# Seven half-size products for the values of four heads, with token forms made in the gelu branch

## The chip, the cores and the metric

The kernel runs on one core of a Trainium2 chip. The metric is the device time of one execution in microseconds. TensorE is written PE, VectorE DVE, ScalarE ACT, GpSimd POOL and SyncE SP, as in the profile.

## The reference

One layer over 528 tokens (16 meta tokens and 512 of the input), model width 1024, all in f32:

```python
h = concat([meta, x]); xn = rms_norm(h, norm_mix_g)
z = xn @ w_in
u_rnn, u_gate, q, k, v, g_ret, ga, gb = split(z)     # 1280, 1280, 1024, 1024, 2048, 2048, 1024, 1024
xr = causal_dwconv(u_rnn); hr = rg_lru(xr)           # two gates per block, then a scan over tokens
o_a = hr * gelu(u_gate)
q, k = rotary(q), rotary(k)                          # 4 heads, dk 256, dv 512
o_b = head_rms(retention(q, k, v)) * silu(g_ret)     # decayed scores, times the values
mixed = sigmoid(ga) * (o_a @ w_branch_rnn) + sigmoid(gb) * (o_b @ w_branch_ret)
h = h + mixed @ w_out
up = causal_dwconv(rms_norm(h, norm_ffn_g) @ w_up); gate, val = split(up)
out = rms_norm(h + (gelu(gate) * val) @ w_down, norm_final_g)[16:]
```

## The kernel before

**Products.** PE multiplies f16. Every f32 operand is cut into a high and a low f16 part (`split`: ACT writes the high part, DVE the low one as source times scale minus high), and a product is made as high x high, high x low and low x high (`SPLIT`, three matmuls). Channels lie on the partitions and tokens along the columns, as `xh`, `xl` for the normed input.

**Weights.** Weights come in units of 128 x 2048 f32. The list `units` gives their order. SP loads a unit into one of two `raw` tiles; its splits are steps that `get()` runs when a unit is needed and `tick()` runs between products, as far ahead as `ahead[0]` allows; a tile of `wsp` holds a split of up to 1024 elements. A plain unit has two splits of 128x1024. A fast unit serves a product of two-by-two blocks by seven half-size products (Strassen-Winograd): two splits of its own blocks (512 and 1024), three sums on DVE (1024, 512 and 512 elements, L256 to L258, which write into `raw`), and two late splits of 1024 (behind ScalarE's last copy). Such products also need four sums of the other operand, its forms, named F3, F5, F6 and F7. `fast_products` does the seven for a gate unit: four psum banks, ACT copies of a bank that is read while it goes on accumulating (`keep`), and DVE additions. ga and gb units and all gates g_ret were fast before the change, as were some of the FFN's.

**Stages on PE**, with their place in the trace: norm and first units to 33 us; the recurrent branch's convolution and gates to 84; the gelu branch, ten projections in the loop `for n in range(NR)`, to 138; between its projections the recurrent branch's gates, exponentials, square roots and scans run on ACT and DVE. Then the rotary projections q0, k0, ... q3, k3 (48 matmuls of 257 or 264 columns each, four psum tiles in turn; DVE gives a tile back with the additions L759 and L760) to 226; the scores and values of the heads, with retention and gates: scores(0) and values(0) from 226, then scores(1), scores(2), values(1), scores(3); from 285 retention_out(0), gated(0), values(2), gated(1), values(3), gated(2), to 420. The mixing (gates ga, gb, branch products, and head 3's gates among them) takes 420 to 690, the output projection to 720, the FFN's first matrix to 948 and its second to 1066.

**values(h).** The weights of a head's values are two plain units of four k blocks by 512 columns. For each of four blocks of 128 tokens, 24 matmuls hold the tokens still and move 512 weight columns (L930). The last 16 tokens have 16 small matmuls over four column groups (L922, `xlast`). Five splits make the values' f16 parts, and `flush()` stands between the blocks.

**make_forms.** The token forms for the gates are made in two halves g around scores(1) and scores(2): per half 12 instructions on DVE and four on ACT, of 514 elements.

**ob_forms.** The second branch's operands are made from the gated retention outputs in three steps for each unit; each step goes to `pending`, and `flush()` takes one. Before, `advance` flushes one after three of the seven products of a gate, `values` after each block.

**Order.** Up to `order.close()`, behind the gelu loop, instructions on an engine run in the order of the code (`manual_schedule`); after it a scheduler orders them per engine.

Of the kernel before, what the change touches and what calls it, by code (L numbers as in the profile page):

```python
# [8 lines left out]
F32 = mybir.dt.float32  # L9
# [17 lines left out]
TQ = T - T0  # L27
FAST_UP = (3, 5, 7, 9)
# [23 lines left out]
def hybrid_block_kernel(ctx, tc, x, meta, norm_mix_g, w_in, conv_w, conv_b, rg_a_w, rg_a_b,  # L52
# [7 lines left out]
    wsp = ctx.enter_context(tc.tile_pool(name="wsp", bufs=10))  # L60
# [67 lines left out]
    def add_v(h):  # L128
        u_v[h] = [unit(4, 512, [(0, 0, kmaj(w_in, 4 * a, 4, o_v + 512 * h, 512))]) for a in range(2)]
# [699 lines left out]
    x_form_t = {}  # L829

    def make_forms(g):

        if not x_form_t:
            for i in range(2):
                x_form_t[i] = xslot([P, 4, 4, 257], F16, f"xs{i}")
        ks = slice(2 * g, 2 * g + 2)
        t = {}
        for i in range(2):
            for j in range(2):
                v = t[i, j] = wtile("xt")[:, :TQ].rearrange("p (k c) -> p k c", k=2)  # L840
                k0, (c0, n) = 4 * j + 2 * g, HQ[i]
                nc.vector.tensor_tensor(v, xh[:, k0:k0 + 2, c0:c0 + n], xl[:, k0:k0 + 2, c0:c0 + n], op=ALU.add)
        a11, a12, a21, a22 = t[0, 0], t[0, 1], t[1, 0], t[1, 1]
        nc.vector.tensor_tensor(a22, a22, a21, op=ALU.subtract)
        nc.vector.tensor_tensor(a21, a11, a21, op=ALU.subtract)
        nc.vector.scalar_tensor_tensor(a11, a22, -1.0, a11, op0=ALU.mult, op1=ALU.subtract)
        nc.vector.scalar_tensor_tensor(a12, a11, -1.0, a12, op0=ALU.mult, op1=ALU.subtract)
        for i, v in enumerate((a12, a22, a11, a21)):
            xs = x_form_t[i // 2]
            split(xs[:, 2 * (i % 2), ks], xs[:, 2 * (i % 2) + 1, ks], v, 1.0)  # L850

    def x_forms(nm, a, k):
        if nm[0] == "A":
            c0, n = HQ[int(nm[1]) - 1]
            return xf(a, 4 * (int(nm[2]) - 1) + k, c0, n)
# [51 lines left out]
    def values(h):  # L907
        vt = []
        wa, wb = get(u_v[h][0]), get(u_v[h][1])
        for b, (j0, nb) in enumerate(JB):  # L910
            if h >= 2 or b % 2 == 0:
                ps = acc("ps")
# [763 lines left out]
```

## Time and profile before

| | |
|---|---|
| median of 3 runs | 1067.75 us (1067.13 to 1067.86) |
| span of the profiled execution | 1066.5 us, 1.25 us below the median of the runs; its mean clock is 0.998 |
| PE busy | 1048.0 us, 98% |
| DVE busy | 853.2 us, 80% |
| ACT busy | 587.9 us, 55% |
| HBM | 108.04 MB read, 103 GB/s over the span |

In the profile a row of groups has line, engine, operation, out<-in, shape and count, then busy time and mean ns of one, then the engine's idle time just before and what ended it. A timeline row has start and length; rows overlap a little where instructions are pipelined, so a pitch is taken from start to start. A number in brackets is idle time before the row and what ended it.

### The profile page before, as it was taken

The page shows a single profiled execution, that of the slowest core. Times are in us where ns is not written, and L with a number is a line of the kernel's source. Part 1 is how long each engine was busy: PE and PEld are TensorE (multiplying, and loading weights), DVE is VectorE, ACT ScalarE, POOL GpSimd, SP SyncE. Part 2 cuts the span into 40 slices and gives each one's busy share as a digit, 9 for nine tenths or more (in the row PEclk, how much of TensorE's full clock was granted, in tenths as well). Part 3 has the DMA queues.
Part 4 walks back from the last instruction along what each step waited for, and adds up shares of the span by engine and source line. Part 5 has one row for each costly group of instructions (what it writes and reads, how often), then busy time and mean ns, then how long its engine had stood idle before and what let it go on. Part 6 is the DMA issues. An engine that isn't in the chain of part 4 may idle for free.

```text
span 1066.5 us, 20995 instructions
## 1 busy us (share of the span) xinstructions
PE 1048.0 (98%) x8995; PEld 851.1 (80%) x8995; DVE 853.2 (80%) x1301; ACT 587.9 (55%) x927; POOL 6.9 (1%) x20
## 2 busy tenths in 40 slices
PE   8999999999999999999999999999999999999997
PEld 6888888865685858887888885588888888888884
DVE  6884799998577878877797776479989897988965
ACT  8568954434364747655554454366566465454442
POOL 2000000000000000000000000000000000000000
PEclk9999999999999999999999999999999999999999
DMA  8341243431022312334433365032432324214322
GB/s 255 104 133 42 80 139 119 160 120 40 2 85 75 120 40 65 119 100 119 129 105 119 115 202 179 1 119 80 159 111 88 119 81 133 67 60 138 101 81 79
DMA packets 108989, 111.49 MB, mean 105 GB/s; under 512 B 5610, under 2 KB 100560, under 8 KB 108896
## 3 DMA queue, kind: packets, MB, share of 16 engines
q1 hardware_dynamic: 108448, 109.74, 32.0%
q8 instruction: 70, 1.15, 0.4%
q10 hardware_dynamic: 160, 0.27, 0.1%
q0 software_dynamic: 288, 0.14, 0.1%
q14 instruction: 23, 0.19, 0.1%
HBM read 108.04 MB, written 2.10 MB: 103 GB/s over the span
## 4 chain that ended last, share of the span: by engine, by line
PE 76%; DVE 13%; ACT 6%; DMA 2%; issue 2%; ACTq 0%; DVEq 0%
PE ps L418 31%; PE P L1512 9%; PE pa L867 7%; PE ps L930 6%; PE ps L1235 4%; DVE wt L93 4%; PE pe L867 3%; PE ps L431 3%; PE pm L418 2%; PE ps L953 2%; PE pa L1399 2%; ACT wt L92 2%; PE pb L867 2%; DVE rnn L665 1%; PE pe L1399 1%
## 5 line engine op out<-in xcount | busy, mean ns | idle before, releaser
L418 PEld LDWEIGHTS <-wt 128*128 128x128 f16 x3840 | 373.2, 97 | 58.2 <-DVE t L759 1.4
L93 DVE SCALAR_TENSOR_TENSOR wt<-raw,wt 128x1024 f16<-128x1024 f32 (+2 forms) x278 | 303.0, 1105 | 58.6 <-ACT wt L92 57.9
L92 ACT ACTIVATE wt<-raw 128x1024 f16<-128x1024 f32 (+2 forms) x278 | 261.4, 962 | 155.7 <-DVE raw L258 30.0
L867 PEld LDWEIGHTS <-wt 128*128 128x128 f16 x2016 | 195.0, 97 | 38.0 <-issue 11.2
L418 PE MATMUL ps<-x2h,wt 128*128 128x258 f16 x1184 | 181.2, 273 | 0.0
L418 PE MATMUL ps<-xh,wt 128*128 128x257 f16 (+2 forms) x1056 | 163.8, 275 | 1.1 <-DVE t L759 1.1
L418 PE MATMUL ps<-x2l,wt 128*128 128x258 f16 x592 | 113.2, 272 | 0.0
L418 PE MATMUL ps<-xl,wt 128*128 128x257 f16 (+2 forms) x528 | 102.2, 275 | 0.0
L1512 PE MATMUL P<-wt,act 128*128 128x256 f16 x792 | 88.3, 273 | 0.0
L1512 PEld LDWEIGHTS <-act 128*128 128x128 f16 x792 | 77.5, 98 | 9.0
L1377 DVE SCALAR_TENSOR_TENSOR cv<-ps,vt,cv 128x512 f32<-128x512 f32 x80 | 59.8, 748 | 22.7 <-ACT cv L1375 21.8
L867 PE MATMUL pa<-xs,wt 128*128 128x257 f16 x576 | 71.6, 273 | 5.1 <-ACT kept L872 4.7
L930 PE MATMUL ps<-wt,xh 128*128 128x512 f16 x256 | 76.1, 379 | 0.4 <-DVE v L93 0.4
L418 PE MATMUL pm<-oa,wt 128*128 128x257 f16 x480 | 55.3, 274 | 0.0
L1375 ACT ACTIVATE cv<-ps,vt,vt 128x512 f32<-128x512 f32 x40 | 30.9, 773 | 34.5 <-PE ps L418 33.8
L930 PE MATMUL ps<-wt,xl 128*128 128x512 f16 x128 | 48.5, 379 | 0.0
L930 PEld LDWEIGHTS <-xh 128*128 128x128 f16 x256 | 24.8, 98 | 29.3 <-issue 0.7
L256 DVE TENSOR_TENSOR raw<-raw 128x1024 f32<-128x1024 f32 x39 | 47.5, 1219 | 0.6
L867 PE MATMUL pa<-ob,wt 128*128 128x257 f16 x384 | 45.7, 274 | 2.0 <-ACT kept L872 1.4
L1235 PE MATMUL ps<-wt,mx 128*128 128x512 f16 x192 | 44.3, 378 | 0.0
L1399 PEld LDWEIGHTS <-wt 128*128 128x128 f16 x336 | 32.6, 97 | 4.4
L1235 PEld LDWEIGHTS <-mx 128*128 128x128 f16 x192 | 17.7, 98 | 18.4
(293 smaller groups left out, 1409.0 us busy)
## 6 DMA issues: line engine op xcount, KB each, us to landing
raw<-in_w_in SPq DMA_DIRECT2D x40, 1024.0 KB, 4.9
raw<-in_w_up SPq DMA_DIRECT2D x24, 1024.0 KB, 5.2
raw<-in_w_down SPq DMA_DIRECT2D x48, 256.0 KB, 3.5
raw<-in_w_branch_ret SPq DMA_DIRECT2D x16, 512.0 KB, 4.7
raw<-in_w_branch_rnn SPq DMA_DIRECT2D x8, 640.0 KB, 4.6
raw<-in_w_out SPq DMA_DIRECT2D x4, 1024.0 KB, 6.2
xin<-in_x SPq DMA_DIRECT2D x4, 512.0 KB, 5.6
raw<-in_w_in SPq DMA_DIRECT2D x4, 512.0 KB, 8.1
```

The costliest lines, as they stand in the source:

```text
L92: a = nc.scalar.activation(hi, src, AF.Copy, scale=s)
L93: b = nc.vector.scalar_tensor_tensor(lo, src, s, hi, op0=ALU.mult, op1=ALU.subtract)
L256: nc.vector.tensor_tensor(pair, pair, rv[:, :, right].rearrange("p (h k) c -> p h k c", h=2), op=ALU.add)
L418: nc.tensor.matmul(ps[:, hf, :n], w(aw, k, col, P), src(ax, k, c0, n), start=k == 0 and (aw, ax) == (0, 0), stop=k == nk - 1 and aw == 1)
L431: mm = nc.tensor.matmul(ps[:, hf, :n], w(aw, k, col, P), src(ax, k, c0, n), start=k == 0 and (aw, ax) == (0, 0), stop=k == KD - 1 and aw == 1)
L867: nc.tensor.matmul(ps[:, :257], ws[k // 4](wf, aw, k % 4), src(xf_, ax, k), start=first and k == 0 and (aw, ax) == (0, 0), stop=k == last_ ...
L930: nc.tensor.matmul(pb, xf(ax, k, XF + j0, nb), w(aw, k % 4, 0, 512), start=i == 0, stop=i == 23)
L1235: nc.tensor.matmul(ps[:, n], mx[k][:, a, c0:c0 + P], wo[k // 2](aw, k % 2, n * 512, 512), start=k == 0 and (a, aw) == (0, 0), stop=k == ks ...
L1375: nc.scalar.activation(vv_, src[:, :, 2:258], AF.Identity, scale=vt2[:, 96 + ch:97 + ch], bias=bias)
L1377: nc.vector.scalar_tensor_tensor(vv_, src[:, :, j:j + 256], vt2[:, 48 * j + ch:48 * j + ch + 1], vv_, op0=ALU.mult, op1=ALU.add)
L1399: nc.tensor.matmul(ps[:, :258], w(wf, aw, k), x2_form(xf_, ax, k), start=first and k == 0 and (aw, ax) == (0, 0), stop=k == 3 and aw == 1, ...
L1512: nc.tensor.matmul(pd[:, 256 * tt:256 * tt + 256], t[:, ax, c0 + tt * P:c0 + tt * P + P], w(wf, aw, i), start=q % 6 == 0 and tt == 0 and i ...
```

## The change

values(h) becomes seven products with fast units, four kept psum regions, three ACT copies and three DVE additions per head. One product is 24 matmuls of 256 columns with a token form held still, 168 per head in place of 96 of 512 columns. The last 16 tokens, which lie outside the two token halves of 256 + 256 in part, get 40 matmuls of 256 columns. The eight units of values become fast units, each loaded by two DMAs of 512 KB in place of one of 1 MB. The token forms widen from 514 to 544 elements and move into the gelu loop, in seven steps after projections 0 to 6; the second half g makes its high parts on DVE. Gates multiply 258 columns instead of 257. The ob forms of heads 0 to 2 wait until the mixing.

```diff
+TH = 256
+TW = T - TH
-    wsp = ctx.enter_context(tc.tile_pool(name="wsp", bufs=10))
+    wsp = ctx.enter_context(tc.tile_pool(name="wsp", bufs=12))
     def add_v(h):
-        u_v[h] = [unit(4, 512, [(0, 0, kmaj(w_in, 4 * a, 4, o_v + 512 * h, 512))]) for a in range(2)]
+        u_v[h] = [unit(4, 512, [(2 * j, 0, kmaj(w_in, 4 * j + 2 * a, 2, o_v + 512 * h, 512)) for j in range(2)], fast=True)
+                  for a in range(2)]
+    def x_form_steps(g, hi_on_vector):
...
+        for i in range(2):
+            for j in range(2):
+                nc.vector.tensor_tensor(v, xh[:, k0:k0 + 2, c0:c0 + TW], xl[:, k0:k0 + 2, c0:c0 + TW], op=ALU.add)
+        yield
+        nc.vector.tensor_tensor(a22, a22, a21, op=ALU.subtract)
+        nc.vector.tensor_tensor(a21, a11, a21, op=ALU.subtract)
+        nc.vector.scalar_tensor_tensor(a11, a22, -1.0, a11, op0=ALU.mult, op1=ALU.subtract)
+        nc.vector.scalar_tensor_tensor(a12, a11, -1.0, a12, op0=ALU.mult, op1=ALU.subtract)
+        yield
+        for i, v in enumerate((a12, a22, a11, a21)):
+            if hi_on_vector:
+                nc.vector.tensor_copy(hi, v)
+                nc.vector.tensor_tensor(lo, v, hi, op=ALU.subtract)
+            else:
+                split(hi, lo, v, 1.0)
+            if i % 2 == 1:
+                yield
+    FORMS = {0: 1, 1: 1, 2: 2, 3: 1, 4: 1, 5: 1, 6: 1}
     for n in range(NR):
...
+        make_forms(FORMS.get(n, 0))
         if n < LAG:
             rnn_gates(NR - LAG + n)
...
     def values(h):
+        def product(ps, wf, xf_, first=False):
+            for a in range(2):
+                for tt in range(2):
+                    for k in range(2):
+                        for ax, aw in SPLIT:
+                            nc.tensor.matmul(ps[:, TH * tt:TH * tt + TH], x_form(xf_, ax, 2 * a + k, tt * P, P),
+                                             ws[a](wf, aw, k), ...
+            tick()
+        product(pa, "B11", "A11", True)
+        first = keep(pa)
+        product(pb, "B21", "A12", True)
+        nc.vector.tensor_tensor(first, pb, first, op=ALU.add)
+        done(0, 0, first, un)
+        product(pe, "T3", "F7", True)
+        product(pa, "T2", "F6")
+        second = keep(pa)
+        product(pa, "T1", "F5")
+        third = keep(pa)
+        nc.vector.tensor_tensor(third, pe, third, op=ALU.add)
+        done(1, 1, third, -un)
+        last = (("B11", xlast, 0, 0), ("B21", xlast, 4, 0), ("T1", xlast, 0, 1), ("B22", xlast, 4, 1), ("B11", xneg, 0, 1))
...
+        product(pa, "B22", "F3")
+        done(0, 1, pa, -un)
+        product(pe, "T4", "A22")
+        nc.vector.tensor_tensor(second, pe, second, op=ALU.add)
+        done(1, 0, second, un)
     def advance(run, *names):
         for nm in names:
             next(run)
-            if nm in ("P7", "P6", "P5"):
+            if not gating[0]:
                 flush()
+    ahead[0] = 8
     scores(0)
     values(0)
-    make_forms(0)
     scores(1)
     scores(2)
-    make_forms(1)
...
-    ahead[0] = 9
+    ahead[0] = 10
```

DVE in the gelu branch between two weight splits, before: `rnn` tiles hold the recurrent branch (L649 multiplies a gate, L658 and L659 form the decay's pair).

```order
L93 SCALAR_TENSOR_TENSOR wt<-raw,wt 128x1024
L649 TENSOR_TENSOR rnn<-rnn,gi 128x528
L93 SCALAR_TENSOR_TENSOR wt<-raw,wt 128x1024
L658 TENSOR_TENSOR a_1440<-rnn 128x528
L659 SCALAR_TENSOR_TENSOR rnn<-a_1440,rnn 128x528
```

The same place now, `xt` being a form in f32 and `xs` its f16 parts:

```order
L95 SCALAR_TENSOR_TENSOR wt<-raw,wt 128x1024
L95 SCALAR_TENSOR_TENSOR xs_1208<-xt,xs_1208 128x544 x2
L95 SCALAR_TENSOR_TENSOR xs_1209<-xt,xs_1209 128x544 x2
L652 TENSOR_TENSOR rnn<-rnn,gi 128x528
L95 SCALAR_TENSOR_TENSOR wt<-raw,wt 128x1024
L728 TENSOR_TENSOR xt<-xh,xl 128x544 x4
L661 TENSOR_TENSOR a_1470<-rnn 128x528
L662 SCALAR_TENSOR_TENSOR rnn<-a_1470,rnn 128x528
```

Steps of the forms now stand in front of the gates and of the decay's pairs. DVE at the end of the rotary stage, before: additions of q3 and k3 (`t`), weight splits, and the first sum of a gate's unit.

```order
L760 TENSOR_TENSOR t_2742<-ps,rope_1851 128x514
L93 SCALAR_TENSOR_TENSOR wt<-raw,wt 128x1024
L761 TENSOR_TENSOR t_2741<-t_2741,t_2742 128x514
L93 SCALAR_TENSOR_TENSOR qk_2626<-t_2736,qk_2626 128x514
L93 SCALAR_TENSOR_TENSOR qk_2627<-t_2741,qk_2627 128x514
L759 TENSOR_TENSOR t_2856<-ps,rope_1850 128x528
L93 SCALAR_TENSOR_TENSOR wt<-raw,wt 128x512
L256 TENSOR_TENSOR raw<-raw 128x2x4x128
L760 TENSOR_TENSOR t_2857<-ps,rope_1851 128x528
L759 TENSOR_TENSOR t_2861<-ps,rope_1850 128x528
L761 TENSOR_TENSOR t_2856<-t_2856,t_2857 128x528
L760 TENSOR_TENSOR t_2862<-ps,rope_1851 128x528
```

And now, L259 to L261 being the sums of a values' unit and L813, L814 the rotary additions:

```order
L95 SCALAR_TENSOR_TENSOR qk_2669<-t_2771,qk_2669 128x514
L95 SCALAR_TENSOR_TENSOR wt<-raw,wt 128x512
L95 SCALAR_TENSOR_TENSOR qk_2670<-t_2776,qk_2670 128x514
L813 TENSOR_TENSOR t_2892<-ps,rope_1892 128x528
L95 SCALAR_TENSOR_TENSOR wt<-raw,wt 128x1024
L259 TENSOR_TENSOR raw<-raw 128x2x2x256
L260 TENSOR_TENSOR raw<-raw 128x2x256
L261 TENSOR_TENSOR raw<-raw 128x2x256
L814 TENSOR_TENSOR t_2893<-ps,rope_1893 128x528
L813 TENSOR_TENSOR t_2897<-ps,rope_1892 128x528
L815 TENSOR_TENSOR t_2892<-t_2892,t_2893 128x528
L814 TENSOR_TENSOR t_2898<-ps,rope_1893 128x528
```

All of a values' unit's split and sums now stand between the first and the second addition on k3's psum tile.

More of the change, by code (lines that the diff above doesn't have):

```diff
@@ L827, in hybrid_block_kernel, with fast_products @@
     vv, oraw, rstd, ob, ob_a11 = {}, {}, {}, [], []
[L829 to L855, printed above, removed]
-        i = ("F3", "F5", "F6", "F7").index(nm)
-        return x_form_t[i // 2][:, 2 * (i % 2) + a, k]
-    def fast_products(ws, src, func, finish):
+    def fast_products(ws, src, func, finish, n=257):
         last_k = 4 * len(ws) - 1
+        c1 = n - 257
         def product(ps, wf, xf_, first=False):
@@ L884, in fast_products @@
         product(pa, "T2", "F6")
[L885 removed]
+        keep(kept[:, h1], pa, c1)
         yield
```

111 lines of the change are left out of this document (69 added, 42 removed).

## The prediction

> **What bounds the kernel now.** I read the page's busy times first, then what TensorE waits for, then busy times by stretch, then the timelines of the stretches that the change touches. TensorE is busy for 98% of the span, and its waits sum to about 12 us, of which one is VectorE's in the rotary stage:
>
> ```profile
> span 1066.5 us, 20995 instructions
> PE 1048.0 (98%) x8995; PEld 851.1 (80%) x8995; DVE 853.2 (80%) x1301; ACT 587.9 (55%) x927; POOL 6.9 (1%) x20
> ```
> ```profile
> engine line waited for: us in total, times, longest us
> PE pa L867 <- ACT kept L872: 6.2, 8, 1.6
> ...
> PE ps L418 <- DVE t L759: 1.1, 1, 1.1
> ...
> PE ps L804 <- DVE krep L793: 0.3, 1, 0.3
> ```
>
> So a product saved is time saved, unless VectorE ends last where it gets more work. The columns below are busy times of PE, PEld, DVE, ACT and POOL, then clock, DMA share and GB/s; the rows are the gelu branch, the rotary stage, its last three quarters, values(2), the gated stages, and the first half of the mixing:
>
> ```profile
> core 0: us, PE busy (x) PEld busy (x) DVE busy (x) ACT busy (x) POOL busy (x), PEclk, DMA share, GB/s
> 92.00:133.05 41.05, 41.05 (x372) 35.88 (x370) 24.86 (x33) 40.75 (x52) 0.00 (x0) 1.00 0.24 78
> 133.10:223.00 89.90, 88.78 (x790) 76.51 (x789) 89.59 (x120) 43.55 (x59) 0.00 (x0) 1.00 0.42 140
> 161.90:229.00 67.10, 67.10 (x595) 57.66 (x594) 65.44 (x92) 29.15 (x40) 0.00 (x0) 1.00 0.47 159
> 320.40:342.20 21.80, 21.80 (x115) 9.64 (x113) 17.64 (x27) 9.78 (x16) 0.00 (x0) 1.00 0.25 84
> 285.50:420.00 134.50, 133.79 (x1145) 98.93 (x1142) 103.28 (x170) 83.00 (x142) 0.00 (x0) 1.00 0.21 69
> 420.00:516.00 96.00, 92.73 (x826) 80.47 (x824) 79.79 (x118) 58.02 (x90) 0.00 (x0) 1.00 0.40 123
> ```
>
> The second row carries the forecast: VectorE idles 0.3 us in 90, while TensorE is nearly as full (its one wait there is 1.1 us). The two finish together, with four psum tiles between them. In the first row VectorE has 41.05 - 24.86 = 16.2 us free, but ScalarE has none.
>
> **The products.** The first two rows are the ends of the 96 products of values(2), then its 16 meta products and the first row of the gate behind; then 72 products of 256 columns in the FFN, which like the new ones change the stationary operand each time; then six products of 16 columns.
>
> ```profile
> 320.36 0.59 PE L930 MATMUL ps<-wt,xh 128*128 128x512 f16 x2
> ...
> 341.18 1.05 PE L922 MATMUL ps<-wt,xlast 128*32 128x512 f16 x16
> 342.16 0.28 PE L867 MATMUL pa<-xh,wt 128*128 128x257 f16 x1
> ...
> 949.86 8.02 PE L1512 MATMUL P<-wt,act 128*128 128x256 f16 x72
> 957.72 1.47 PE L1512 MATMUL P<-wt,a 128*128 128x256 f16 x12
> ...
> 285.37 0.30 PE L804 MATMUL ps<-qk,krep 128*128 128x16 f16 x6
> 285.52 0.68 PE L953 MATMUL ps<-sc,v 128*128 128x257 f16 x6
> ```
>
> One 512-wide product takes (341.18 - 320.36) / 96 = 0.217 us, one 256-wide (957.72 - 949.86) / 72 = 0.109. Per head 20.82 us becomes 168 x 0.1092 = 18.34: -2.48, and **-9.9 us** for four heads. The Trainium skill (TensorE: Matmul & The Clock Gate, "Back-to-back issue gap") speaks against this saving: it gives a sustained 131 ns for load-and-multiply pairs at 512 columns and 81 ns at 128, whereby the 96 would take only 12.6 us and the 168 at least 13.6, an estimate of +4 us in place of -9.9. The rows above, which change the stationary each time, show 217 and 109, so the row decides.
>
> The meta tokens: 16 products of 512 columns take 342.16 - 341.18 = 0.98 us, 61 ns each; 40 of 256 columns replace them. If columns count, 31 ns each (1.2 us); if the instruction counts, 61 (2.4); no lower than the 25 ns of the six 16-wide ones (1.0). I take 45 ns, 1.8 us, between those ends: +0.8 per head, **+3.2** (0 to +6). The gates' 258 columns in place of 257 add 1 column in 1344 products, 0.109/256 each: **+0.3** on average between nothing and +0.6.
>
> **VectorE up to the end of the rotary stage.** The forms are 28 instructions of 544 elements on VectorE: 12 for g=0, whose four hi parts ScalarE makes, and 16 for g=1, whose hi parts VectorE casts. Their nearest rows, and those of splits and sums:
>
> ```profile
> 130.78 2.35 DVE L93 SCALAR_TENSOR_TENSOR wt<-raw,wt 128x1024 f16<-128x1024 f32 x2
> 133.05 0.70 DVE L664 TENSOR_TENSOR rnn<-rnn 128x528 f32<-128x528 f32 x1
> ...
> 224.53 0.69 DVE L93 SCALAR_TENSOR_TENSOR wt<-raw,wt 128x512 f16<-128x512 f32 x1 [1.27 <-ACT wt L92]
> 225.26 1.22 DVE L256 TENSOR_TENSOR raw<-raw 128x1024 f32<-128x1024 f32 x1
> ...
> 228.41 0.70 DVE L760 TENSOR_TENSOR t<-ps,rope 128x528 f32<-128x528 f32 x1
> ...
> 237.89 1.89 DVE L842 TENSOR_TENSOR xt<-xh,xl 128x514 f32<-128x514 f16 x3
> 239.70 0.22 DVE L793 COPY krep<-qk 128x256 f16<-128x256 f16 x1
> ```
>
> Three form additions of 514 take 239.70 - 237.89 = 1.81 us, 0.603 each; with 544 elements about 0.635 each, so 28 x 0.635 = 17.8 us. The old place (the same instructions around 236 to 271 us) cost TensorE next to nothing, since of its waits only 0.3 us stood there: leaving it saves nothing. A split of 1024 has a pitch of (133.05 - 130.78) / 2 = 1.14 us, so a plain unit costs VectorE 2 x 1.14 = 2.3; a fast unit costs 0.61 + 3 x 1.14 for the splits and 1.2 + 2 x 0.61 for the sums, 6.4 less what overlaps: about +4.1 for each of the eight value units. Counting the new order up to the addition that gives back the last rotary psum tile (in the trace the one at 228.41), the fast units put 7.1 us into this stretch, and 1.2 of other work slides behind it: 17.8 + 7.1 - 1.2 = **23.7 us more** between 92 and 229.
>
> What can that hide in? The 16.2 us free before 133, and 1.27 at 224.5. Nothing else: from 133 to 223 VectorE is full. If all 17.5 is filled, VectorE is 6.2 late at 229. But the pauses are waits for ScalarE, which is full there and gets four more hi splits (about 0.6 each, +2.2 us); whatever VectorE does meanwhile, the exponentials come no sooner:
>
> ```profile
> 108.03 1.23 DVE L93 SCALAR_TENSOR_TENSOR wt<-raw,wt 128x1024 f16<-128x1024 f32 x1 [3.36 <-ACT wt L92]
> 112.00 0.71 DVE L658 TENSOR_TENSOR a<-rnn 128x528 f32<-128x528 f32 x1 [2.74 <-ACT rnn L656]
> ...
> 111.23 3.24 ACT L656 ACTIVATE rnn<-rnn,cneg 128x528 f32<-128x528 f32 x5
> ```
>
> The forms stand in seven lumps, the first of four (2.5 us) in a pause of about 3.3; where a lump is longer than its pause (the second additions in front of the decay pairs, say) it delays the decay, and the square roots and scans behind it. I take 11 to 11.5 us filled, two thirds. VectorE then reaches the first scan (133 before) 6 to 7 us late, the rotary tiles are given back later, TensorE stalls first at q0/q1 (4 to 6 us), and, since VectorE needs longer than TensorE from there on too, again at scores and values of head 0: 12.4 late at 229. TensorE now takes that tile at 229.84, 0.7 us after VectorE gives it back (228.41 + 0.70), so of these 12.4, **+11.7 us** reach it. Bounds: 6.2 - 0.7 = +5.5 with every pause filled, +15 with 8 us filled. The Trainium skill (VectorE: DVE Perf Modes, "The perf-mode tier table") has f32 copies in SBUF at twice the rate of two-source operations, by which the four casts would be an estimated 1.1 us cheaper in all; the trace has only an f16 copy (0.22 us at 256), which doesn't settle it.
>
> **From there on.** In values(0) VectorE has room again (waits of 1 to 3 us around 244 to 250), so the lateness doesn't grow; ScalarE's three kept copies and VectorE's additions per head, in front of products that reuse the bank, put some waits in: **+1.0** (0 to 3). In the gated stages VectorE has 31 us free of 134.5; the five remaining fast units (+20) fit, the more as the ob forms leave. What those cost there is small: TensorE waits 134.5 - 133.79 = 0.7 us in all, so taking the ob forms out gains at most that. The first and last of their eight groups between 300 and 425 us, which sum to 24.1 us busy, some 20 in pitch:
>
> ```profile
> L93 DVE SCALAR_TENSOR_TENSOR ob<-y,ob 128x514 f16<-128x514 f32 x6 | 4.1, 685 | 0.0
> ...
> L1005 DVE TENSOR_TENSOR y<-d,or 128x257 f32<-128x257 f32 x6 | 2.5, 419 | 0.0
> ```
>
> They go between the gates of the mixing, where VectorE has 16.2 us free of 96. One more unit prepared ahead takes out about 6.4, so 79.8 + 20 - 6.4 = 93 of 96: nearly full, behind gates whose ScalarE copies hold TensorE up already (96 - 92.73 = 3.3 us of waits). **+1.5** (0 to +5).
>
> **Sum.** +11.7 - 9.9 + 3.2 + 0.3 + 1.0 + 1.5 = +7.8. The sum stands against the profiled execution, whose span of 1066.5 lies 1.25 under the median of 1067.75; that difference stays. Forecast 1067.75 + 7.8 = **1075.5 us**. A difference under 0.2%, 2.1 us, can't be told from none.
>
> **Rivals.**
> - *The forms fit the pauses (faster).* All idle time of the gelu branch is filled, so +5.5 is left, meta products cost 31 ns (+1), and no other waits come: 5.5 - 9.9 + 1 + 0.3 = -3.1, 1064.6. For it: 16.2 us free, and lumps of the size of the pauses. Against: ScalarE has 0.3 us free in 41. It decides once VectorE comes to 229 less than 7 us late: chance 0.13.
> - *Only the first stall (near the same).* TensorE stalls 6 us at q0/q1 and VectorE keeps pace after: 6 - 9.9 + 3.2 + 0.3 + 1 + 1 = +1.6, 1069.4. Against: 65.44 of 67.10 us are taken before anything is added. Chance 0.15, half of it within 0.2%.
> - *The mixing becomes VectorE's.* The lateness as forecast, and +5 or more between the gates: 1080 to 1083. For it, 93 of 96; against, the forms are needed only by the second branch's products. Chance 0.13.
> - *Weight loads bound the new products.* One load of 97 ns stands beside 109 ns of columns; with 5 ns over, 168 x 4 x 0.005 = +3.4 more. Against: the 72 products above load as often at 109. Chance 0.05. The skill's page on TensorE ("LDWEIGHTS") puts a load at 107 ns, closer still; the row L867 below shows 97.
> - The forecast, +5 to +11: the remaining 0.54.
>
> ```profile
> L867 PEld LDWEIGHTS <-wt 128*128 128x128 f16 x2016 | 195.0, 97 | 38.0 <-issue 11.2
> ```
>
> Leaving out at most 2 in 10, the range goes from 1067 (most of the faster case left out) to 1081. Faster 0.13, same 0.08, slower 0.79.
>
> **What would show it.** Right: new waits of TensorE on VectorE's rotary additions at q0/q1 and again at scores or values of head 0, about 10 to 14 us together; VectorE without pauses from 100 to 240; values(2) at 20.2 us in place of 21.8. Wrong: first scan before 137 us, no wait at head 0's scores (then the second step fails), meta products far from 45 ns, or waits of more than 5 us between the gates.

## The result and the profile after

The changed kernel takes 1081.61 us (median of 4, 1081.18 to 1083.32) against 1067.8 of the kernel before in the same comparison: ratio 1.013, 95% interval 1.0116 to 1.0145. It is 13.8 us slower, on the side that was forecast, but 0.6 us above the range and with 6.0 us more than the forecast 7.8. Now and then an execution ran at a clearly lower clock: the profile of e5 is of one (mean clock 0.75), and the ratio of e11 has one of 1100.33 us in it.

The page after, first its span and busy times, then TensorE's waits (total, times, longest):

```profile
span 1079.7 us, 21841 instructions
PE 1048.3 (97%) x9379; PEld 884.5 (82%) x9379; DVE 896.1 (83%) x1358; ACT 600.8 (56%) x951; POOL 6.9 (1%) x20
```
```profile
PE pa L892 <- ACT kept L897: 7.0, 9, 2.4
PE pa L892 <- ACT last L897: 4.1, 4, 1.2
PE ps L421 <- DVE wt L95: 2.5, 1, 2.5
PE ps L421 <- DVE t L813: 2.4, 1, 2.4
PE ps L858 <- DVE t L813: 2.3, 1, 2.3
...
PE ps L858 <- DVE krep L847: 1.4, 2, 0.8
```

Against before, the waits on VectorE's rotary additions grow from 1.1 to 4.7 us, a wait for a weight split (2.5) and one for `krep` (1.4 in place of 0.3) come in, and the waits on ScalarE's copies grow from 6.7 (6.2 and 0.5) to 11.1. TensorE's busy time is as large as before although products were saved; the clock is one reason, as the windows show. The first two rows answer to the gelu branch and rotary rows of before; the other two are stretches of some 3.4 us behind two of the waits:

```profile
core 0: us, PE busy (x) PEld busy (x) DVE busy (x) ACT busy (x) POOL busy (x), PEclk, DMA share, GB/s
92.00:140.00 48.00, 48.00 (x434) 41.97 (x433) 42.26 (x62) 47.68 (x63) 0.00 (x0) 1.00 0.21 67
140.00:240.00 100.00, 92.54 (x789) 77.72 (x786) 99.76 (x134) 40.15 (x56) 0.00 (x0) 0.97 0.37 122
153.80:157.10 3.30, 3.30 (x17) 2.33 (x16) 3.30 (x5) 0.00 (x0) 0.00 (x0) 0.52 0.67 226
242.30:245.70 3.40, 3.40 (x19) 2.35 (x17) 3.24 (x10) 1.71 (x5) 0.00 (x0) 0.50 0.00 0
```

VectorE, which idled 16.2 us in the 41 us ahead of the first scan, idles 5.7 in 48, and then 0.2 us in a hundred. Behind the waits the granted clock is about 0.5 for 3.4 us, which is called half clock from here on: TensorE does 1.7 us less of its work in that time. The timeline has the waits in brackets; then the first scan on VectorE (133.05 before) and the addition that gives back the last rotary tile (228.41 before):

```profile
152.53 0.63 PE L421 MATMUL ps<-xh,wt 128*128 128x264 f16 x4 [2.50 <-DVE wt L95]
...
167.27 0.59 PE L421 MATMUL ps<-xh,wt 128*128 128x257 f16 x2 [2.43 <-DVE t L813]
...
239.23 0.55 PE L858 MATMUL ps<-qk,qk 128*128 128x144 f16 x6 [2.30 <-DVE t L813]
240.59 0.23 PE L858 MATMUL ps<-qk,krep 128*128 128x16 f16 x3 [0.82 <-DVE krep L847]
240.68 0.38 PE L952 MATMUL pv<-wt,xh 128*128 128x256 f16 x2
```
```profile
139.88 0.70 DVE L667 TENSOR_TENSOR rnn<-rnn 128x528 f32<-128x528 f32 x1
...
239.70 0.70 DVE L814 TENSOR_TENSOR t<-ps,rope 128x528 f32<-128x528 f32 x1
```

Five points on TensorE's timeline make a ledger. The first row has their times before, the others how much later each came:

| profiled execution | first product of values(0) | retention_out(0) | end of values(3) | output projection | span |
|---|---|---|---|---|---|
| before | 229.84 | 285.52 | 390.98 | 649.52 | 1066.5 |
| change | +10.8 | +10.8 | +10.0 | +13.2 | +13.2 |

The output projection runs from 649.5 to 696 us before the change, so the mixing ends at 649.5 and not at 690.

### The profile page after: what moved, and what is told of

The parts are those of the page before. It is cut to its first block, busy times and chain, and to the rows that moved or that the text cites. A ratio compares the mean times of both kernels' runs of the same rounds, so it can differ in the third digit from the quotient of the medians.

```text
span 1079.7 us, 21841 instructions
## 1 busy us (share of the span) xinstructions
PE 1048.3 (97%) x9379; PEld 884.5 (82%) x9379; DVE 896.1 (83%) x1358; ACT 600.8 (56%) x951; POOL 6.9 (1%) x20
## 4 chain that ended last, share of the span: by engine, by line
PE 67%; DVE 23%; ACT 7%; issue 2%; DMA 1%; ACTq 0%; DVEq 0%
PE ps L421 25%; PE P L1571 9%; DVE wt L95 7%; PE pa L892 7%; PE ps L1294 4%; PE pv L952 3%; PE ps L434 3%; PE pe L892 2%; ACT wt L94 2%; PE pa L1458 2%; PE pm L421 2%; PE pb L892 2%; PE ps L1014 2%; DVE raw L259 2%; PE pa L952 2%
## 5 line engine op out<-in xcount | busy, mean ns | idle before, releaser
L95 DVE SCALAR_TENSOR_TENSOR wt<-raw,wt 128x1024 f16<-128x1024 f32 (+2 forms) x294 | 318.7, 1098 | 49.6 <-ACT wt L94 49.1
L94 ACT ACTIVATE wt<-raw 128x1024 f16<-128x1024 f32 (+2 forms) x294 | 273.6, 954 | 153.1 <-DVE raw L261 37.1
L421 PE MATMUL ps<-xh,wt 128*128 128x257 f16 (+2 forms) x1056 | 166.1, 278 | 4.9 <-DVE wt L95 2.5
L892 PE MATMUL pa<-xs,wt 128*128 128x258 f16 x576 | 71.1, 273 | 9.7 <-ACT kept L897 7.0
L1436 DVE SCALAR_TENSOR_TENSOR cv<-ps,vt,cv 128x512 f32<-128x512 f32 x80 | 59.9, 748 | 20.2 <-ACT cv L1434 19.2
L259 DVE TENSOR_TENSOR raw<-raw 128x1024 f32<-128x1024 f32 x47 | 57.3, 1220 | 0.6
L952 PEld LDWEIGHTS <-xs 128*128 128x128 f16 x384 | 37.4, 98 | 7.4 <-issue 3.2
L260 DVE TENSOR_TENSOR raw<-raw 128x512 f32<-128x512 f32 x47 | 32.3, 688 | 0.8
L261 DVE TENSOR_TENSOR raw<-raw 128x512 f32<-128x512 f32 x47 | 32.3, 688 | 0.8
```

The costliest lines, as they stand in the source:

```text
L94: a = nc.scalar.activation(hi, src, AF.Copy, scale=s)
L95: b = nc.vector.scalar_tensor_tensor(lo, src, s, hi, op0=ALU.mult, op1=ALU.subtract)
L259: nc.vector.tensor_tensor(pair, pair, rv[:, :, right].rearrange("p (h k) c -> p h k c", h=2), op=ALU.add)
L260: nc.vector.tensor_tensor(rv[:, low, right], rv[:, top, left], rv[:, low, right], op=ALU.add)
L421: nc.tensor.matmul(ps[:, hf, :n], w(aw, k, col, P), src(ax, k, c0, n), start=k == 0 and (aw, ax) == (0, 0), stop=k == nk - 1 and aw == 1)
L892: nc.tensor.matmul(ps[:, :n], ws[k // 4](wf, aw, k % 4), src(xf_, ax, k), start=first and k == 0 and (aw, ax) == (0, 0), stop=k == last_k ...
```

## The experiments

All runs are below, with their ratio to the kernel before (and its interval), then the same ledger: how late values(0) starts and values(3) ends, and the length of the stretch from there to the output projection, 258.5 us before. The last two columns take that stretch apart: TensorE's idle time in it (7.1 us before) and what half clock took in it (nothing before); the rest, its products at full clock, is 251 us in every row, give or take 0.5 (252.3 in e11). Two executions of much the same kernel differ in the stretch (258.5 before, 257.2 and 257.3 in e14 and e17), mostly by one wait of 1.4 us on a copy at 640.9; so 1.4 us is how far one execution is to be trusted there.

| run | median us | ratio | values(0) | end of values(3) | stretch behind | idle in it | half clock in it |
|---|---|---|---|---|---|---|---|
| change | 1081.61 | 1.0130 (1.0116 to 1.0145) | +10.8 | +10.0 | 261.7 | 10.5 | 0 |
| e1 no forms | 1074.98 | 1.0072 (1.0057 to 1.0087) | +3.9 | +2.6 | 263.1 | 10.1 | 1.7 |
| e2 no sums | 1075.29 | 1.0083 (1.0068 to 1.0098) | +7.7 | +4.8 | 262.9 | 10.3 | 1.7 |
| e3 operands as before | 1083.80 | 1.0157 (1.0142 to 1.0172) | +10.8 | +11.6 | 262.0 | 9.1 | 1.7 |
| e4 all three | 1070.22 | 1.0031 (1.0019 to 1.0044) | +0.7 | -1.8 | 262.2 | 9.0 | 1.7 |
| e5 before, VectorE +1.9 | 1073.65 | 1.0059 (1.0036 to 1.0082) | | | | | |
| e6 before, VectorE +4.0 | 1073.70 | 1.0054 (1.0037 to 1.0071) | +7.1 | +7.1 | 260.2 | 7.3 | 1.7 |
| e7 before, limits and tiles | 1074.08 | 1.0055 (1.0038 to 1.0072) | +1.3 | +1.6 | 262.4 | 9.2 | 1.7 |
| e8 two heads, 12 tiles | 1077.06 | 1.0088 (1.0068 to 1.0107) | +1.3 | +3.2 | 264.1 | 11.3 | 1.7 |
| e9 old limits | 1082.37 | 1.0142 (1.0127 to 1.0157) | +11.4 | +11.6 | 261.4 | 10.2 | 0 |
| e10 products alone | 1071.03 | 1.0034 (1.0021 to 1.0047) | +0.7 | -1.2 | 262.5 | 9.6 | 1.7 |
| e11 two operand steps | 1085.52 | 1.0218 (1.0147 to 1.0290) | +11.1 | +10.2 | 265.2 | 12.9 | 0 |
| e12 forms on GpSimd | 1079.22 | 1.0110 (1.0095 to 1.0126) | +8.7 | +8.2 | 261.3 | 10.1 | 0 |
| e13 before, 12 tiles | 1073.43 | 1.0056 (1.0042 to 1.0069) | +1.2 | +1.5 | 262.3 | 9.3 | 1.7 |
| e14 before, new limits | 1067.04 | 0.9998 (0.9989 to 1.0007) | 0.0 | 0.0 | 257.2 | 5.9 | 0 |
| e15 10 tiles, old limits | 1078.92 | 1.0102 (1.0088 to 1.0115) | +8.8 | +7.9 | 261.4 | 8.7 | 1.7 |
| e16 two heads, late operands | 1070.15 | 1.0024 (1.0014 to 1.0033) | +0.2 | -1.0 | 260.8 | 9.6 | 0 |
| e17 before, small scratch | 1066.99 | 0.9999 (0.9990 to 1.0008) | -0.1 | -0.1 | 257.3 | 6.0 | 0 |
| e18 two heads, 10 tiles | 1073.19 | 1.0058 (1.0043 to 1.0072) | +0.2 | +1.1 | 262.7 | 10.2 | 1.7 |

**The forms, the sums, the operands (e1 to e4).** e1 leaves the forms out:

```diff
-        return x_form_t[i // 2][:, 2 * (i % 2) + a, k, c0:c0 + n]
+        return xf(a, 4 * (i // 2) + k, XF + TH * (i % 2) + c0, n)
...
-        make_forms(FORMS.get(n, 0))
```

> The changed kernel without making the token forms (28 VectorE and 4 ScalarE instructions left out; the products read slices of the tokens themselves instead, so the output is not the reference's). Theory A, VectorE's lateness at the end of the rotary stage costs the time: 17.8 of the 23.7 us added there go, the rest fits the pauses; values of head 0 start at most 2 us later than before (229.8) instead of 10.8, no wait over 1.5 us at q0/q1 or at the scores of head 0, no drop of the granted clock in 150 to 250 us: 1067 to 1070. Rival B, the price lies in the values' products and between the gates of the mixing: at most 4 us are gained, 1077 or more.

Measured: values(0) starts 6.9 us earlier than in the change, the time falls from 1.0130 to 1.0072 of before, about 6.2 us, which lies between the theories. Theory A has the place right, its amount was too large: values(0) is still 3.9 us late (sums and tiles), half clock still comes behind the waits at the scores of head 0 (234.2 to 237.6 us), and the stretch behind values(3) gives nothing back.

e2 leaves the sums of the values' units out:

```diff
         def sums():
+            if no_sums:
+                return
...
```

> The changed kernel in which the values' units leave out their three sums (1024, 512 and 512 elements per unit, about 2.4 us of VectorE; output not the reference's). Theory A: three units' sums, 7.2 us, stand before the end of the rotary stage, so the start of head 0's values moves from 10.8 us late to about 4, and the time to 1073 to 1076. Rival B: the sums lie in VectorE's free time: 1080 to 1082.

Measured: values(0) at +7.7, not +4, for 3.1 us of the 7.2 taken out ahead of it. Yet 5.0 us are gained in all, as theory A had it: 1.5 more come in values(0) and values(1), where the clock stays at full speed, since the wait at the scores is gone with a part of the lateness, and 0.6 in the gated stages. (The profiled execution took 1077.32 us, the other three 1075.19 to 1075.30; it loses 1.2 behind values(3).)

e3 flushes the second branch's operands as before the change:

```diff
+                if not gating[0]:
+                    flush(3)
...
-            if not gating[0]:
+            if nm in ("P7", "P6", "P5"):
                 flush()
...
     gated(2)
+    flush(3)
     gating[0] = False
```

> The changed kernel with the second branch's operands flushed as before the change (after three of seven products of every gate from head 0 on). Theory A: the 3.2 us that arise between the end of gated(2) and the output projection come from these 20 us of VectorE work between the gates, and go: 1078 to 1079. Rival B: VectorE in the gated stages now carries the values' fast units too, and pays the same there: 1081 to 1083. Rival C: ScalarE's copies make the waits in the mixing whatever VectorE does: 1081 to 1082 with the same waits on the copies.

Measured: 2.9 us slower (1.0157 against 1.0130), rival B and a little more. values(2) takes 21.8 us and values(3) 22.5 where the change has 20.8, waiting for VectorE's weight splits: in the gated stages the new place is needed. The stretch behind is no shorter, but its parts differ: TensorE idles 9.1 us there instead of 10.5, and half clock, which the change doesn't have there, takes 1.7. So the operands' new place costs the mixing some 1.4 us of waits, hardly more than one execution differs from the next, and theory A of the operands has less than half of its 3.2.

e4 takes the three out together.

> The three edits together: no token forms, no sums for the values' units, operands of the second branch as before (output not the reference's). What remains of the change is the products. Theory A: four heads at about 1.0 to 1.7 us saved, nothing else lost: 1061 to 1064. Rival B (products of half size do not pay with their waits): 1066 or more.

Measured: at the end of values(3) the kernel is 1.8 us ahead of before, so the four heads save 2.5 where theory A has 4 to 6.8. The stretch behind is 3.6 us longer than before all the same, 1.9 of it idle time and 1.7 half clock, and the kernel ends 0.3% slower, in rival B's range. Something that none of the three edits touches costs this.

**The clock (e5, e6).** The kernel before gets idle work on VectorE behind its last scan, two additions in e5 and five in e6:

```diff
+    late_t = wtile("lt")
+    nc.vector.memset(late_t, 0.0)
+    for _ in range(5):
+        nc.vector.tensor_add(late_t, late_t, late_t)
     oa = {}
```

> The kernel before with one memset and two dependent additions of 128x528 more on VectorE behind the last scan, about 1.9 us, which nobody uses. TensorE's wait at q1 grows from 1.1 to about 3.0 us. Theory A (a wait of about 2.4 us or more halves the granted clock for 3.4 us, which costs 1.7 us more where VectorE then isn't the last): granted clock near 0.83 in the 10 us behind the wait, time 3 to 4 us above before. Rival B (the clock holds): 1.2 to 2 us above before, clock 1.00.

> The same with five additions, about 4.0 us in all. Theory A: wait of about 5 us, the same 3.4 us at half clock, 5 to 6 us above before. Rival B: 3.3 to 4.2 us above before.

From e6's profile, the wait at q1 and the 5.2 us behind it:

```profile
166.08 0.61 PE L418 MATMUL ps<-xh,wt 128*128 128x257 f16 x2 [5.21 <-DVE t L764]
```
```profile
166.07:171.24 5.17, 5.16 (x25) 3.62 (x26) 5.17 (x9) 2.96 (x5) 0.00 (x0) 0.50 0.02 3
```

Measured: e5 is 6.3 us slower than before, e6 5.8. In e6's profile the one wait that changed grew by 5.21 - 1.12 = 4.1 us, and values(0) starts 7.1 later; 2.6 of the other 3.0 us are lost to the clock, which is 0.50 for the 5.2 us behind the wait. That is theory A's mechanism. The profiled execution took 1076.90 us, the other four 1073.08 to 1073.80; by the median, 5.8 - 4.1 = 1.7 us go beyond the wait, the amount that I gave it. e5's 6.3 us are above both theories. Its five other executions had a mean clock of 0.995 (the middle one), those of before one of 0.998: an estimate of (0.998 - 0.995) x 1072 = 3.2 us, which with 1.9 us of added work leaves about 1 us open. Where that clock was lost its profile can't tell.

The Trainium skill (TensorE: Matmul & The Clock Gate, "What's actually happening") has the clock halved after an idle window of some 3.4 us that runs free. The half clock and its 3.4 us agree with the rows above. The waits that set it off were shorter, 2.3 to 2.5 us in the change, and one of 2.4 us in the mixing of the change left the clock at 1.00.

So the length of a wait doesn't decide it alone. The profiles here, e5's left out, have 30 waits of TensorE of 2.0 to 2.9 us between 100 and 1000 us; half clock came behind 21 of them, and not behind nine. The stretches of half clock begin at 153.56, 167.22 and 242.31 us in the change, 4 and 22 times 3.413 us apart, and such whole multiples lie between the stretches of every profile that has more than one. On this grid, these are the 3.41 us ahead of the three stretches, then the two windows on which the wait of 2.4 us at 527 us falls:

```profile
150.15:153.56 3.41, 1.02 (x9) 0.89 (x10) 3.41 (x5) 0.00 (x0) 0.00 (x0) 1.00 0.00 0
163.80:167.22 3.42, 1.04 (x10) 0.65 (x7) 3.42 (x6) 2.15 (x3) 0.00 (x0) 1.00 0.00 0
238.89:242.31 3.42, 1.69 (x20) 1.17 (x21) 3.42 (x8) 1.29 (x2) 0.00 (x0) 1.00 0.00 0
...
522.20:525.61 3.41, 2.70 (x25) 2.24 (x23) 2.69 (x4) 3.41 (x6) 0.00 (x0) 1.00 0.04 12
525.61:529.03 3.42, 1.75 (x16) 1.56 (x16) 3.42 (x6) 1.85 (x5) 0.00 (x0) 1.00 0.86 294
```

TensorE was busy for 1.02, 1.04 and 1.69 us of the windows ahead of half clock, and for 2.70 and 1.75 of the other two: a wait within one window (or, in the third, with the two `krep` waits behind it) was followed by half clock, one that two windows share was not. In the 15 profiles with such stretches, every window with under 1.4 us of busy time was followed by half clock, and none with over 1.7 unless the clock was at half already.

**Limits, tiles, scratch (e7, e9, e13, e14, e15, e17).** To the kernel before come, in e7, all three of the change's settings:

```diff
-    wsp = ctx.enter_context(tc.tile_pool(name="wsp", bufs=10))
+    wsp = ctx.enter_context(tc.tile_pool(name="wsp", bufs=12))
...
+    ahead[0] = 8
     scores(0)
...
-    ahead[0] = 9
+    ahead[0] = 10
...
+    ahead[0] = 9
...
-    nc = bacc.Bacc("TRN2", target_bir_lowering=False, num_devices=1)
+    nc = bacc.Bacc("TRN2", target_bir_lowering=False, num_devices=1, dynamic_dma_scratch_size=4096)
```

The last pair is the smaller DMA scratch that pays for the tiles; e13 has tiles and scratch, e14 the limits, e17 the scratch.

> The kernel before with the change's limits on preparing ahead (8, 10 and 9), its 12 split tiles and its smaller DMA scratch, nothing else. Theory A (ScalarE's copies stand behind weight splits that come in another phase): waits on the copies in 390 to 650 us rise as in the change, 2 to 4 us slower than before. Rival B: the phase in the mixing is set by the values' units, and the limits alone do nothing: within 1 us of before.

> The kernel before with 12 split tiles in place of 10 (and the smaller DMA scratch that makes room for them), nothing else. Theory A (the ten tiles held the splits back, so that fewer stood in front of the gates' copies): most of the 6 us of e7, 1071 to 1074, the stretch from the end of values(3) to the output projection 261 to 263 us. Rival B (the limits do it): 1067 to 1068, that stretch 258 to 259 us.

> The kernel before with the change's limits on preparing ahead (8, 10, 9) and its own 10 tiles. Theory A (the tiles do it): 1067 to 1069. Rival B: 1071 to 1074, with the krep waits of 1.2 us at the scores of head 0 that e7 shows.

> The kernel before with the smaller DMA scratch alone. Theory A (the tiles make the 6 us of e13, by letting one more low part go ahead of a unit's sums): 1066.5 to 1068.5, same waits as before. Rival B (the scratch does it): 1071 or more.

Measured: e7 5.9 us slower, e13 6.0, e14 and e17 nothing. So it is the two additional split tiles, which I had given no term. In e13, values(0) starts 1.2 us later, behind `krep` waits at the scores of head 0 (a weight split goes in ahead of the last rotary additions), and the stretch behind values(3) is 3.8 longer, 2.1 of it idle time and 1.7 half clock. There its longest wait reads so, ScalarE first, then VectorE, then TensorE:

```profile
516.21 1.06 ACT L92 ACTIVATE wt<-raw 128x1024 f16<-128x1024 f32 x1 [3.36 <-DVE raw L256]
517.17 0.37 ACT L872 ACTIVATE kept<-pa 128x257 f32<-128x257 f32 x1
...
510.89 4.09 DVE L93 SCALAR_TENSOR_TENSOR wt<-raw,wt 128x1024 f16<-128x1024 f32 x4
514.90 1.22 DVE L256 TENSOR_TENSOR raw<-raw 128x1024 f32<-128x1024 f32 x1
...
517.59 2.74 PE L867 MATMUL pa<-xs,wt 128*128 128x257 f16 x12 [2.62 <-ACT kept L872]
```

The same place before, some 2 us earlier:

```profile
511.68 0.39 ACT L872 ACTIVATE kept<-pa 128x257 f32<-128x257 f32 x1 [0.27 <-PE pa L867]
513.22 1.06 ACT L92 ACTIVATE wt<-raw 128x1024 f16<-128x1024 f32 x1 [1.15 <-DVE raw L256]
...
508.91 2.95 DVE L93 SCALAR_TENSOR_TENSOR wt<-raw,wt 128x1024 f16<-128x1024 f32 x3
511.90 1.22 DVE L256 TENSOR_TENSOR raw<-raw 128x1024 f32<-128x1024 f32 x1
...
512.81 1.49 PE L867 MATMUL pa<-xs,wt 128*128 128x257 f16 x12
```

ScalarE takes its instructions one after the other. In e13 a split's high part waits there for VectorE's sum, VectorE makes four low parts ahead of that sum where it made three, and the gate's first copy, for which TensorE waits, stands behind the split. Before, that copy (511.68) came ahead of the split, and TensorE went on at 512.81 without a wait. In e13 the clock halves on top of it, from 517.35 us on.

For the change itself, e9 has the old limits and e15 the old limits and 10 tiles.

> The changed kernel with the limits on preparing ahead of the kernel before (6 until scores(3), 9 in the gated stages and the mixing). Theory A (the limits brought weight splits in front of the gates' copies, and two units more of VectorE work in front of the rotary's end): head 0's values start earlier than 10.8 us late, the copies' waits in the mixing fall, 1075 to 1079. Rival B (with 4-tile value units the phase is off with either set of limits): 1080 to 1084.

> The change with 10 split tiles and the old limits. Theory A (tiles): the stretch behind values(3) goes from 261.7 to 258 to 260 us, waits in values(0) for tiles may come, 1077 to 1081. Rival B (any other phase of the splits costs the same): 1081 to 1084, that stretch at 261 or more.

Measured: e9 is no quicker than the change, rival B. e15 is 4.3 us below e9 by the ratios, with theory A's time and rival B's stretch: values(0) starts 2.6 us earlier, values(0) and values(1) gain 0.9, and the stretch behind values(3) stays at 261.4. That it stays is chance. These are the stretches of the change, e3, e9 and e15, with TensorE's busy time first and the clock third from the end:

```profile
400.97:662.69 261.72, 251.19 (x2266) 218.60 (x2264) 220.88 (x328) 150.24 (x239) 0.00 (x0) 1.00 0.36 114
402.55:664.53 261.98, 252.83 (x2266) 219.38 (x2264) 210.49 (x304) 145.84 (x227) 0.00 (x0) 0.99 0.36 114
402.53:663.93 261.40, 251.19 (x2266) 218.62 (x2264) 220.77 (x328) 150.34 (x239) 0.00 (x0) 1.00 0.37 114
398.88:660.23 261.35, 252.66 (x2267) 219.43 (x2265) 223.06 (x329) 150.80 (x239) 0.00 (x0) 0.99 0.37 118
```

With 10 tiles TensorE idles 8.7 us there, in e9 10.2, and half clock behind a wait of 2.25 us takes what was gained, where e9's wait of 2.44 us left the clock alone. So the tiles account for some 1.5 us of waits in the mixing of the change, hardly more than one execution differs from the next.

**What else lengthens the mixing (e10, e11).** e10 is e4 with the old limits; e11 takes two operand steps for each product between the gates.

> No token forms, no sums for the values' units, the second branch's operands and the limits as before the change (output not the reference's): the seven products and the value units' five splits are what is left. Theory A (limits cost about 3 us in the mixing): 1064 to 1067, stretch from the end of values(3) to the output projection 258 to 260 us as before. Rival B (the value units' own splits shift the phase): that stretch stays at 262 us, 1068 to 1071.

> The changed kernel in which the second branch's operands are made two steps for each product between the gates instead of one, so that no lump is left in front of gate_b's copies. Theory A (ScalarE's copy of a gate's bank stands behind five of those steps' high parts, and TensorE waits 2.4 us at 527 us): that wait goes, 1079 to 1080. Rival B: the steps only move in front of other copies, 1081 to 1083.

Measured: e10 is rival B, the stretch stays at 262.5, with 2.4 us more idle time than before and 1.7 of half clock. e11 is slower than the change, past rival B: 1085.5 us, the stretch 265.2, with new waits on VectorE's gate additions (2.6). The rows behind e11, in the change:

```profile
521.83 2.52 ACT L94 ACTIVATE wt<-raw 128x1024 f16<-128x1024 f32 x3 [1.89 <-DVE raw L261]
524.26 0.62 ACT L94 ACTIVATE ob<-y 128x514 f16<-128x514 f32 x1
...
526.87 0.36 ACT L897 ACTIVATE kept<-pa 128x257 f32<-128x257 f32 x1
...
527.28 1.48 PE L892 MATMUL pa<-xs,wt 128*128 128x258 f16 x12 [2.38 <-ACT kept L897]
```

Three splits that waited 1.9 us for VectorE's sum and five operand parts stand in front of the copy: the same queue as in e13. With the operands as before (e3, e4, e10) the waits of 2 to 3 us stand at other copies, at 486 or 499 us. Each tried arrangement of splits and operands has its copies caught behind something, for 1.6 to 5.8 us of idle time over before, and in eight of the thirteen half clock takes 1.7 more. Which edit sets off which wait in the change was not taken apart further, and no run has four heads with 10 tiles and the operands in their old place.

**GpSimd (e12).** The plain additions and differences of the forms, and the second half's casts and low parts, go to GpSimd:

```diff
-                nc.vector.tensor_tensor(v, xh[:, k0:k0 + 2, c0:c0 + TW], xl[:, k0:k0 + 2, c0:c0 + TW], op=ALU.add)
+                nc.gpsimd.tensor_tensor(v, xh[:, k0:k0 + 2, c0:c0 + TW], xl[:, k0:k0 + 2, c0:c0 + TW], op=ALU.add)
...
```

> The changed kernel with 20 of the 28 instructions of the token forms on GpSimd (additions, plain differences, and the second half's casts and low parts), which is idle 99% of the span. Theory A (VectorE's load sets the lateness at 230 us): 12.7 us leave VectorE, head 0's values start 0 to 5 us late instead of 10.8 where GpSimd is quick enough, 1071 to 1077. Rival B (VectorE's remaining steps wait for GpSimd, or both slow each other at the same memory): 1080 or more.

```profile
L728 POOL TENSOR_TENSOR xt<-xh,xl 128x544 f32<-128x544 f16 x8 | 10.9, 1366 | 79.2 <-DVE rnn L652 62.5 <-PE ps L421 16.1 <-DVE xs L95 0.7
L741 POOL TENSOR_TENSOR xs<-xt,xs 128x544 f16<-128x544 f32 x4 | 7.0, 1760 | 0.2
...
PE 1047.3 (97%) x9379; PEld 884.0 (82%) x9379; DVE 893.5 (83%) x1338; ACT 601.1 (56%) x951; POOL 35.2 (3%) x40
```

Measured: 1.37 to 1.76 us on GpSimd for what takes 0.72 on VectorE, and values(0) starts only 2.1 us earlier (+8.7). The time lies between the theories, just under rival B's, and the mechanism is rival B's second one. Four low parts of the forms on VectorE, in e12 with one of GpSimd's additions beside them, then in the change:

```profile
102.29 5.42 DVE L95 SCALAR_TENSOR_TENSOR xs<-xt,xs 128x544 f16<-128x544 f32 x4 [0.32 <-ACT xs L94]
101.61 1.43 POOL L728 TENSOR_TENSOR xt<-xh,xl 128x544 f32<-128x544 f16 x1 [0.73 <-PE ps L421]
...
102.19 2.62 DVE L95 SCALAR_TENSOR_TENSOR xs<-xt,xs 128x544 f16<-128x544 f32 x4
```

VectorE takes twice as long for them. Over the gelu branch its instructions that run beside GpSimd's are 9.9 us longer than the same ones in the change, and so its busy time falls from 896.1 us to 893.5 only, though 20 instructions have left it. ScalarE's instructions there are no longer than in the change.

**Two heads (e8, e16, e18).** Heads 0 and 1 keep plain units and products of 512 columns, and the forms go back around scores(1) and scores(2):

```diff
-    values(0)
+    plain_values(0)
+    make_forms(0)
     scores(1)
     scores(2)
+    make_forms(1)
-    values(1)
+    plain_values(1)
...
```

> Seven products for heads 2 and 3 alone; heads 0 and 1 with plain units and 512-wide products, the token forms made around scores(1) and scores(2), the second branch's operands and the limits on preparing ahead as before; gates with 258 columns and 12 split tiles as in the change. Theory A: nothing is added before 230 us, so the lateness there is none; values(2) and values(3) save 1.0 us each, the gates' copies give back 1 us, the mixing up to 3: 1066 to 1070. Rival B: VectorE's extra splits and sums for heads 2 and 3 (about 16 us) make TensorE wait in the gated stages: above 1070.

> Seven products for heads 2 and 3 alone, forms around scores(1) and scores(2), old limits, 10 tiles, but the second branch's operands made between the gates as in the change, so that VectorE is free for the fast units. Theory A: each of values(2) and values(3) is 1.0 us shorter than 21.8 (in e8 they were 21.8 and 22.6), and at most 1 us is given back in the mixing: 1064 to 1067. Rival B (the mixing's phase costs 3 us or more, as in e8): 1069 to 1073.

> Seven products for heads 2 and 3, old limits, 10 tiles, the second branch's operands as before the change. Theory A (VectorE, with splits, sums and operands together, is late for the value units in the gated stages): values(2) and values(3) stay at 21 to 22.5 us in place of 20.8, 1069 to 1074. Rival B (with 10 tiles the units are ready): 20.8 us each, 1065 to 1067.

Measured: nothing is late at values(0) in any with 10 tiles. With late operands (e16) values(2) and values(3) take 20.8 us each in place of 21.8, theory A's half, but the stretch behind is 2.3 us longer, all of it idle time: 0.24% slower than before, in rival B's range of time. With the operands in the gated stages (e8, e18) VectorE is late for the value units (21.6 and 22.3 us in e18), and TensorE waits 5 us for one copy in the mixing: rival B of e8, theory A of e18. No version of the seven products here beats the kernel before.

## Why the prediction was partly right

**The lateness: right in size, with one stall not forecast.** VectorE reached the first scan 6.8 us late (6 to 7 forecast) and the last rotary addition at 239.70, 11.3 us late (12.4). TensorE stalled at q1 and again at the scores of head 0, as forecast, and took values(0) 10.8 us late (11.7). Its first stall, 2.50 us at k0, was for a weight split and not for a rotary addition. The waits sum to 8.6 us where 10 to 14 were to be the sign; half clock behind the first two, 1.7 us each, makes up most of the rest of the lateness, and costs nothing beyond it, since VectorE, with hardly a pause there, comes last. Of the 16.2 us of pauses 10.5 were filled (11 to 11.5 forecast). That neither the forms nor the sums alone make it is shown by e1 (-6.9) and e2 (-3.1). A part of it, 1.2 us on the kernel before and 2.6 in the change (e13; e15 against e9), came from the two tiles, of which the prediction says nothing.

**The casts.** Their pitch is 0.48 us beside 0.64 of the low part behind (0.44 in length beside 0.72). The Trainium skill (VectorE: DVE Perf Modes, "The perf-mode tier table") gave twice the rate; the trace has them 1.3 times as quick by the pitch and 1.6 by the length, so the four are some 0.6 us cheaper:

```profile
126.34 0.44 DVE L740 CAST xs<-xt 128x544 f16<-128x544 f32 x1
126.82 0.72 DVE L741 TENSOR_TENSOR xs<-xt,xs 128x544 f16<-128x544 f32 x1
127.46 0.43 DVE L740 CAST xs<-xt 128x544 f16<-128x544 f32 x1
```

**The products: right in size, wrong in what they leave.** values(2) in the change:

```profile
342.85 0.62 PE L985 MATMUL pv<-wt,xlast 128*32 128x256 f16 x15
343.66 2.78 PE L952 MATMUL pa<-wt,xs 128*128 128x256 f16 x24 [0.20 <-ACT kept L960]
...
346.37 0.71 PE L985 MATMUL pv<-wt,xlast 128*16 128x256 f16 x17
346.82 0.48 PE L985 MATMUL pv<-wt,xneg 128*32 128x256 f16 x8
347.23 2.79 PE L952 MATMUL pa<-wt,xs 128*128 128x256 f16 x24
349.86 0.38 PE L952 MATMUL pe<-wt,xh 128*128 128x256 f16 x2
```

24 products take 349.86 - 347.23 = 2.63 us, 0.110 each, as forecast. The meta products take 0.81 us in front of 343.66, 0.2 of it a wait, and 0.86 in front of 347.23: 1.47, 37 ns each (45 forecast). The whole takes 20.8 us (20.2 forecast, 21.8 before), so about 0.9 us per head goes to waits and gaps. The step that failed is "**From there on**": it allowed +1.0 us for the waits of all four heads together. Between the ledger's points, heads 0 and 1 save 0.0 where 2.9 was forecast (2 x (2.48 - 0.8) less half of the 1.0); 1.7 of the difference is the clock's: 3.4 us at 0.5 in values(0), where TensorE is the last; e2 and e4, with the clock at full speed there, save 1.5. Heads 2 and 3 save 0.8 with the gates between them where 2.7 was forecast (the same, less half of the gates' 0.3): each of the two values stages saves 1.0, and the copies of the gates between them take two waits of 0.5 us where before had none.

**The clock was in no term.** Behind the stall at the scores of head 0 it costs its 1.7 us in full.

**The mixing: mis-sized.** +1.5 was forecast and +3.2 measured (+4.5 against e14 and e17, without the one wait of 1.4 us in the profile of before), inside its bounds of 0 to 5, but not for the reason that was given. VectorE is less full than forecast, busy for 93.00 of the 100 us from 420 on where the estimate was 93 of 96. The waits are ScalarE's queue, in which copies stand behind splits that wait for VectorE. The limits don't make them (e9, e14). The operands' place (e3) and the tiles (e15) account for some 1.5 us each, each hardly beyond what one execution differs from the next; the rest stays open. On the kernel before, two tiles alone cost 6.0 us (e13), an edit to which the prediction gave no term.

The misses against the forecast are -0.9 us for the lateness, +2.9 and +1.9 for the heads, +1.7 for the mixing, and 0.65 between median and span (1.9 us now, 1.25 before): about +6.2, against 13.8 - 7.8 = 6.0 measured.

**The rivals.** The one that had 5 us or more between the gates named the time that came, 1080 to 1083, by luck: the mixing took 3.2, and the rest was lost in the heads' products. The two faster rivals needed VectorE less than 7 us late or no second stall, and both came otherwise. Weight loads did not bound the new products, at 0.110 us each.

## What to carry to other kernels

Where two engines finish a stage together, work added to the one that isn't the bound is paid in full beyond the pauses it can fill; about two thirds of pauses that wait for a third engine could be filled here (10.5 of 16.2 us). Count with half clock behind a stall of TensorE of 2 to 3 us: it came behind 21 of 30 here, for 3.4 us or twice that, and 3.4 us of it cost 1.7 where nothing else was late. Before you compare the length of a stage in two runs, take the half clock out: it hid a gain of some 1.5 us in e3 and in e15. And cost a change of buffer counts like an edit of the order: more buffers let work go ahead that a short buffer had held back, and on an engine that takes its work in order it can go in front of what the bound engine waits for.

## What the runs showed of the hardware that I had not expected

Waits of TensorE of 2.0 to 2.9 us brought the granted clock to 0.5 for 3.4 or 6.8 us in 21 cases of 30, by where they fell on a grid of 3.413 us; one of 5.2 us brought 6.8 us (e6), and the one of 1.1 us in the profile of before left the clock at 1.00. GpSimd took 1.37 us for the addition of 128x544 that takes VectorE 0.72, and 1.76 for an f32 and f16 difference, and VectorE took 5.42 us beside it for four instructions that take 2.62 without it. Meta products of 256 columns on 32-column stationaries went at 37 ns each where 512 columns took 61.
